# One RWKV-7 / gMLP layer: TensorE's sequence in the pair rounds fixed as the program traces it, with stated delays

## The chip, the cores and the metric

The kernel runs on one core of a Trainium2 chip, in one launch. The metric is the time of one execution on the device in microseconds (us). Two runs of the kernel before took 1193.26 and 1194.86 us, median 1194.06.

## What is computed

One layer of a decoder is applied to 512 prompt rows and 8 x 4 sample rows (544 rows in all, 1024 channels). Cut to what matters here:

```
xn   = rmsnorm(h);  proj = xn @ w_in            # columns [r | k | v | u | v_g | gate_A | gate_B], 7168 in all
r,k,v = token-shift mix of the first 3072 columns
decay, a, g = low-rank (LoRA) products of token-shifted xn
kk   = k * k_k / |k * k_k| (per head);  k = k * (1 + (a - 1) * k_a)
per head (16 of 64 channels), per row:          # RWKV-7 scan
    sa = S @ -kk;  S = S * w + sa (x) (kk * a) + v (x) k;  y = S @ r
o_A  = (head_norm(y) + sum(r * k * r_k) * v) * g
o_B  = gelu(u) * chunk_mix(layernorm(gelu(v_g)))
h   += rmsnorm((sigmoid(gate_A) * o_A + sigmoid(gate_B) * o_B) @ w_out)
h   += rmsnorm(relu(rmsnorm(h) @ w_up)^2 @ w_down);  h += sigmoid(h @ w_pg) * (p @ w_pe)
```

## The kernel before, in words

Channels lie on the 128 partitions and rows along the free axis, as eight tiles of 128 channels. A **dense** product (`dense`, L209 to 215, matmul at L214) of one 128x128 weight tile column with 544 rows is made in two halves of up to 296 and 258 columns. Each of 8 k-steps takes three matmuls: weights and rows are both split in a high and a low part (`xh`, `xl`, `w_hi`, `w_lo`; L188 to 193). A dense tile is thus 48 matmuls. `wload` (L195) reads its weights by SyncE and splits them on ScalarE (L191) and VectorE (L192).

The scan works on **pairs of heads**, p = 0 to 7, one tile of 128 channels each, and on eight chunks of 64 rows. These are the stages, each a Python generator that yields an estimate of its TensorE time:

- `front(p)` (L395 to 549): the dense k, r and v tiles (`rkv`, L321), the inverse norm of k per head, the LoRA products, exponentials, and the chunk products M (`L486`), BKT, ZV (the "products").
- `solve(p)` (L605): inverts each chunk's triangular matrix by 28 dependent VectorE steps between small products. scr (M to DRAM, L504), Xi (back, L612), solved (L623) and XD (L627) go through DRAM.
- `chain(p)` (L677): the scan over the chunks; each needs the last. A chunk is three hops: px = ZV^T M (L687), copied as Xc by ScalarE (L691); TT^T Xc (L701), read by ScalarE (L702) and VectorE (L703) into ZV; BKT^T ZV (L706), read by VectorE (L717) into the next chunk's ZV. L689 and L707 collect the outputs in py.
- `samples(p)` (L552): the sample rows, in small products.
- `back(p)` (L727): head norm of the output Y, gate g. `gates(p)` (L755): two dense gate tiles, and the result's sum. `mlp_u(j)` (L998): the dense u tiles.

A per-head sum is two matmuls with 0/1 weights on a split operand (`head_sum`, L339; matmuls L349, 350). `head_inverse` (L353) takes such sums as two rows, sends them by DMA to 64 partitions (st, L361, GpSimd's queue), takes 1/sqrt there and sends the result back (invk for k, invy for the head norm, L369, GpSimd's queue); `head_spread` (L373, matmul L377) spreads it over the heads' channels by two matmuls.

In **round** p (loop at L1111, p from -1 to 8) `weave` (L813) interleaves chain(p), samples(p), solve(p+1), front(p+2), back(p-1) and the gates that GATES names, always taking the generator that is furthest behind its share of the round in SPAN. That gives the program's order, and each instruction's priority. The tile scheduler then orders every engine's instructions itself, from priorities and its own estimates of when operands are ready. "Small products" below are matmuls of 64 rows or columns or less, which use a part of TensorE's array.

```
        def weave(*items):
            ...
            while live:
                x = min((x for x in live if len(x[2]) < 5 or x[2][4]()), key=lambda x: x[0])
```

After the rounds, w_out, w_up, w_down and w_pg follow as dense products.

Of the kernel before, what the change touches and what calls it, by code (L numbers as in the profile page):

```python
# [9 lines left out]
F32 = mybir.dt.float32  # L10
# [17 lines left out]
EARLY = ()  # L28

SPAN = {"chain": (0, 0.55), "samples": (0.1, 0.8), "solve": (0.05, 1.2), "front": (0, 1), "u": (-0.05, 1.04),  # L30
        "back": (-0.1, 0.5), "gates": (0, 1), "mixed": (0.4, 0.83), "front0": (0.1, 1.15), "mix": (0.3, 0.8),
        "u0": (0.1, 1.09)}
# [111 lines left out]
def _program(tc, a, o):  # L144
    nc = tc.nc
    act, dve, pe, sp, gp = nc.scalar, nc.vector, nc.tensor, nc.sync, nc.gpsimd
    from contextlib import ExitStack
# [38 lines left out]


# [108 lines left out]
    with tc.tile_pool(name="dr", bufs=1, space=DRAM) as dr:  # L296
# [24 lines left out]
        def rkv(kind, p, pad=0):  # L321

            w = wload(a["win"][8 * "rkv".index(kind) + p])
            t = ew.tile([128, 640 if pad else NT], F32, name=kind, tag=kind, bufs=2 if kind == "k" else 1)
            pa, pb = pd("d"), pd("d")
            dense(pa[:, 0:296], w, X, (0, 296))
            dense(pb[:, 0:258], w, X, (294, 552))
# [9 lines left out]
            return t  # L337

        def head_sum(x, sel, m, ring, tag):  # L339

            out = []
            for c0, c1 in (SA, SB):
# [5 lines left out]
                p_ = pd(ring)[0:m, 0:n]  # L348
                pe.matmul(p_, lhsT=sel, rhs=hi[:, 0:n], start=True, stop=False)  # L349
                pe.matmul(p_, lhsT=sel, rhs=lo[:, 0:n], start=False, stop=True)  # L350
                out.append(p_)
            return out

        def head_inverse(pool, sq, norm, tag, ring):

            rows = ew.tile([2, NT], F32, name="rows", tag="rows", bufs=1)
            for (c0, c1), p_ in zip((SA, SB), head_sum(sq, selw, 2, ring, tag)):
                act.copy(out=rows[:, c0:c1], in_=p_)  # L358
# [36 lines left out]
        def front(p):  # L395
            s = S[p]
            k = rkv("k", p)
            yield 5.6
            sq = ew.tile([128, NT], F32, name="sq", tag="tmp", bufs=1)
            act.activation(out=sq, in_=k, func=AF.Square, scale=vcol("k_k", p))  # L400
            inv = head_inverse(ew, sq, (1e-24, ALU.max, 1.0, ALU.mult), "k", "s")
# [39 lines left out]
            yield 1  # L441

# [5 lines left out]
            yield 1  # L448
            if p == 0:
# [24 lines left out]
            r_ = rkv("r", p)  # L474
            yield 5.6
# [4 lines left out]
            yield 0.5  # L480

# [9 lines left out]
            yield 3.5  # L491
# [18 lines left out]
            BKT = pair_tile(p, "BKT", [128, 8, 128], 2)  # L510
            for c in range(0, 8, 4):
# [4 lines left out]
                act.copy(out=BKT[:, c:c + 4], in_=p_.rearrange("p (c t) -> p c t", c=4))  # L516
            BKTs = ew.tile([128, 64], F32, name="BKTs", tag="BKTs", bufs=2)
# [5 lines left out]
            v = rkv("v", p, 32)  # L523
            yield 5.6
            ZV = pair_tile(p, "ZV", [128, 9, 2, 64], 2)
            SV = ew.tile([128, 64], F32, name="SV", tag="SV", bufs=2)
            for c in (0, 4, 8):
# [7 lines left out]
                else:  # L535
# [3 lines left out]
                    else:  # L539
                        act.copy(out=ZV[:, 0:3, 1], in_=q_[:, 1:4, 1])  # L540
                if c == 0:
# [3 lines left out]

            sv = pair_tile(p, "sv", [128, NT], 3)
            for (c0, c1), p_ in zip((SA, SB), head_sum(r_, blk, 128, "s", "v")):
                dve.tensor_tensor(out=sv[:, c0:c1], in0=p_, in1=v[:, 32 + c0:32 + c1], op=ALU.mult)
            yield 1
            s.update(F=Fp, KR=KR, M=M, scr=scr, BKT=BKT, ZV=ZV, sv=sv, KRs=KRs, Ms=Ms, BKTs=BKTs, SV=SV, Fs=Fs)  # L550

# [822 lines left out]
```

## Time and profile before

| | before |
|---|---|
| median of 2 runs | 1194.06 us |
| the profiled execution | 1195.11 us, its span 1193.3 us |
| before pair 0's front | 0 to about 95 us of the span |
| the rounds | about 95 to 690 us |
| w_out to the end | about 690 to 1193 us |
| TensorE, VectorE, ScalarE busy | 97%, 68%, 49% |

Busy shares are of the whole span. Durations of matmuls in the trace are from a matmul's start to its modelled end, which can lie past the start of the next; distances of starts tell how many a stretch can hold. Rows are those of the profiled execution, whose own time is the one to set a sum against.

### The profile page before, as it was taken

The numbers are of one execution on the slowest core, as the hardware profiler recorded it, in microseconds if no ns is written. First come the engines' busy times: TensorE is split into PE (matmuls) and PEld (weight loads), VectorE is DVE, ScalarE is ACT, GpSimd is POOL, SyncE is SP. The second block draws the span as 40 slices with busy tenths as digits, with TensorE's granted clock in tenths as the row PEclk, the third lists the DMA queues.
The fourth block names the chain that finished last, engine by engine and source line by source line (L and its number), as shares of the span: only waits on it lengthen the run. The fifth ranks groups of instructions, "written<-read, shape, count | busy, mean of one in ns | idle before, by whom it ended". The sixth has DMA issues, their size and how long they took to land.

```text
span 1193.3 us, 26307 instructions
## 1 busy us (share of the span) xinstructions
PE 1159.7 (97%) x10262; PEld 1086.1 (91%) x10262; DVE 815.6 (68%) x2251; ACT 579.7 (49%) x1406; POOL 108.0 (9%) x199
## 2 busy tenths in 40 slices
PE   7999998999899999999999999999999999999998
PEld 7999997888788888888878998999999999999998
DVE  6795778687878888887876646844563464465584
ACT  6646336557474747464655546642232232233352
POOL 0000012202230221122110000000000000000000
PEclk9999999999999999999999999999999999999999
DMA  6243253211222123141331452222222222222322
GB/s 203 72 126 114 100 159 114 86 50 46 63 74 83 48 64 99 34 118 44 112 95 55 131 171 72 91 81 89 88 89 89 89 89 89 89 89 89 116 73 83
DMA packets 68236, 109.33 MB, mean 92 GB/s; under 512 B 13712, under 2 KB 19760, under 8 KB 68112
## 3 DMA queue, kind: packets, MB, share of 16 engines
q1 hardware_dynamic: 60224, 103.94, 27.6%
q0 software_dynamic: 7600, 3.50, 1.8%
q8 instruction: 81, 1.33, 0.5%
q14 instruction: 43, 0.35, 0.1%
q10 hardware_dynamic: 288, 0.21, 0.1%
HBM read 94.40 MB, written 13.00 MB: 90 GB/s over the span
## 4 chain that ended last, share of the span: by engine, by line
PE 72%; DVE 12%; DMA 7%; ACT 6%; issue 2%; SPq 1%; POOL 0%; DVEq 0%; ACTq 0%; POOLq 0%
PE ps_d L214 47%; PE ps_s L214 3%; PE ps_s L486 2%; PE ps_b L214 2%; PE ps_m L214 2%; DVE w_lo L192 2%; ACT w_hi L191 2%; PE ps_cx L687 1%; PE ps_cx L701 1%; PE ps_cx L706 1%; DMA w_raw<-in_wout 1%; DMA w_raw<-in_wpg 1%; PE ps_cy L707 1%; DVE KR L456 1%; PE ps_m L601 1%
## 5 line engine op out<-in xcount | busy, mean ns | idle before, releaser
L192 DVE TENSOR_TENSOR w_lo<-w_raw,w_hi 128x512 fp32r<-128x512 f32 (+1 forms) x288 | 195.5, 681 | 174.0 <-ACT w_hi L191 169.9
L191 ACT CAST w_hi<-w_raw 128x512 fp32r<-128x512 f32 (+1 forms) x288 | 176.2, 613 | 275.9 <-PE ps_d L214 190.1
L214 PE MATMUL ps_d<-xh,w_hi 128*128 128x256 f32 (+3 forms) x832 | 249.4, 300 | 3.5 <-ACT w_hi L191 2.5
L214 PE MATMUL ps_d<-xl,w_hi 128*128 128x256 f32 (+3 forms) x832 | 246.9, 297 | 0.0
L214 PE MATMUL ps_d<-xh,w_lo 128*128 128x256 f32 (+3 forms) x832 | 246.9, 297 | 0.0
L214 PE MATMUL ps_d<-hh,w_hi 128*128 128x288 f32 (+1 forms) x1200 | 227.7, 288 | 0.0
L214 PEld LDWEIGHTS ps_d<-hh,w_hi 128*128 128x128 f32 x1200 | 188.8, 188 | 0.0
L214 PE MATMUL ps_d<-hh,w_lo 128*128 128x288 f32 (+1 forms) x600 | 173.6, 289 | 0.0
L214 PEld LDWEIGHTS ps_d<-xh,w_hi 128*128 128x128 f32 x832 | 157.5, 189 | 7.5 <-ACT w_hi L191 2.9
L214 PEld LDWEIGHTS ps_d<-xl,w_hi 128*128 128x128 f32 x832 | 157.6, 189 | 4.0 <-issue 3.2
L214 PEld LDWEIGHTS ps_d<-xh,w_lo 128*128 128x128 f32 x832 | 157.1, 189 | 2.2 <-issue 0.8
L214 PE MATMUL ps_d<-ax,w_hi 128*128 128x288 f32 (+1 forms) x704 | 133.3, 288 | 0.0
L214 PEld LDWEIGHTS ps_d<-hh,w_lo 128*128 128x128 f32 x600 | 112.8, 188 | 0.2 <-DVE w_lo L192 0.2
L214 PEld LDWEIGHTS ps_d<-ax,w_hi 128*128 128x128 f32 x704 | 110.3, 188 | 0.4 <-issue 0.2
L214 PE MATMUL ps_d<-ax,w_lo 128*128 128x288 f32 (+1 forms) x352 | 101.5, 288 | 0.0
L214 PEld LDWEIGHTS ps_d<-ax,w_lo 128*128 128x128 f32 x352 | 66.2, 188 | 0.0
L1256 ACT ACTIVATE ax<-t 128x288 fp32r<-128x288 f32 (+1 forms) x64 | 27.5, 430 | 45.4 <-DVE t L1255 45.2
L214 PE MATMUL ps_d<-gx,w_hi 128*128 128x288 f32 (+1 forms) x192 | 41.4, 309 | 6.8 <-ACT gx L853 6.0
L697 ACT ACTIVATE ZP<-ZV,Fp 64x64 f32<-64x64 f32 x96 | 33.1, 345 | 20.7 <-DVE ZV L717 17.3
L214 PEld LDWEIGHTS ps_d<-gx,w_hi 128*128 128x128 f32 x192 | 32.3, 199 | 8.1 <-ACT gx L853 6.0
L1257 DVE TENSOR_TENSOR t<-t 128x288 f32<-128x288 f32 (+1 forms) x64 | 28.1, 439 | 15.7 <-ACT ax L1256 15.3
L361 POOL DMA_DIRECT2D st<-rows x32 | 16.2, 511 | 243.9 <-ACT rows L358 176.8
(455 smaller groups left out, 2295.4 us busy)
## 6 DMA issues: line engine op xcount, KB each, us to landing
w_raw<-in_win SPq DMA_DIRECT2D x112, 256.0 KB, 2.8
w_raw<-in_wup SPq DMA_DIRECT2D x64, 256.0 KB, 2.7
w_raw<-in_wdn SPq DMA_DIRECT2D x64, 256.0 KB, 2.8
w_raw<-in_wout SPq DMA_DIRECT2D x16, 256.0 KB, 3.1
w_raw<-in_wpg SPq DMA_DIRECT2D x16, 256.0 KB, 2.9
w_raw<-in_lora SPq DMA_DIRECT2D x10, 256.0 KB, 2.8
xt<-in_xt SPq DMA_DIRECT2D x8, 276.0 KB, 5.4
ud<-u SPq DMA_DIRECT2D x8, 272.0 KB, 2.2
```

The costliest lines, as they stand in the source:

```text
L191: act.copy(out=hi, in_=raw)
L192: dve.tensor_tensor(out=lo, in0=raw, in1=hi, op=ALU.subtract)
L214: pe.matmul(out, lhsT=w[wi][k - k0], rhs=x[xi][k][:, cols[0]:cols[1]], start=start and n == 0 and j == 0, stop=stop and n == len(ks) - 1 a ...
L361: gp.dma_start(out=st[32 * h:32 * h + 32], in_=rows[h:h + 1].rearrange("o (a b) -> o a b", b=17))
L456: dve.tensor_tensor(out=KR[r, :, 0, h], in0=c3(kk)[r], in1=E[r, :, 0:64], op=ALU.mult)
L486: pe.matmul(p_[:, 256 * ci:256 * ci + 256], lhsT=BK[:, c + ci].rearrange("p a t -> p (a t)"), rhs=KR[:, c + ci].rearrange("p a h t -> p (a ...
L601: pe.matmul(p_[r], lhsT=s["BKTs"][r], rhs=SX[r], start=True, stop=True)
L687: pe.matmul(px[:, 0:128], lhsT=flat(M[:, c, 0]), rhs=flat(ZV[:, c]), start=True, stop=True)
L697: act.activation(out=ZP[r], in_=zv[h][r], func=AF.Copy, scale=F[r, c + 1, 0:1])
L701: pe.matmul(px[:, 0:128], lhsT=TT[:, c], rhs=Xc, start=True, stop=True)
L1256: act.activation(out=hi, in_=t, func=AF.Square)
L1257: dve.tensor_tensor(out=t, in0=t, in1=t, op=ALU.mult)
```

## The change

1. TensorE's instructions in the rounds are taken from the tile scheduler: `tc.manual_schedule(engines={PE})` keeps them in the order in which the program emits them. The other engines are still ordered by the scheduler; the chain's instructions get high priority there.
2. A class `Clock` stands in for TensorE while the program is traced and adds up an estimated time. Generators may yield `(cost, delay)`: `weave` resumes them only when that clock has passed the delay. HOP, 1.5 us, is the delay after each hop of the chain and the samples.
3. All dense tiles of the rounds come from one stream, `tiles()`, two k-steps (six matmuls, `dense_by`) at a time. Weights are loaded one tile ahead. `weave` emits a dense piece when the round's quota of tiles is behind the furthest-behind ready generator, or when no generator is ready. In front, back and gates the dense tiles are no longer inside the generator; `until` waits for what a tile or another generator sets.
4. `products` is split from `front` and emitted one round later. `head_sum` puts 3 us between its split and its matmuls, with one at a time under way (`held`). The spread of invk is held 11 us, that of invy 17; solve's steps 6, 14, 7 and 3 us.
5. rows -> st goes by ScalarE's queue in place of GpSimd's. u tiles 4 and 5 stand in round -1, 6 and 7 in rounds 6 and 7.

```diff
-EARLY = ()
+U = {-1: (4, 5), 6: (6,), 7: (7,)}
+HOP = 1.5
+    class Clock:
+        def matmul(self, out, lhsT, rhs, **kw):
...
+            self.now += t + (0.17 if small != self.small else 0)
+            return nc.tensor.matmul(out, lhsT=lhsT, rhs=rhs, **kw)
+    pe = Clock()
+    def dense_by(out, w, x, cols, by=2):
+        for k in range(0, KT, by):
+            dense(out, w, x, cols, ks=range(k, k + by), k0=0, start=k == 0, stop=k + by == KT)
+            yield 0.37 * by
+        def until(q, what):
+            while q >= 0 and not S[q].get(what):
+                yield 0, 0.3
-        def head_sum(x, sel, m, ring, tag):
+        def head_sum(x, sel, m, ring, done):
+            while held[0]:
+                yield 0, 0.2
+            held[0] = True
...
+            yield 0, 3
+            held[0] = False
...
-                gp.dma_start(out=st[32 * h:32 * h + 32], in_=rows[h:h + 1].rearrange("o (a b) -> o a b", b=17))
+                act.dma_start(out=st[32 * h:32 * h + 32], in_=rows[h:h + 1].rearrange("o (a b) -> o a b", b=17))
         def front(p):
-            k = rkv("k", p)
-            yield 5.6
+            yield from until(p, "k")
+            k = s["k"]
...
+            yield 0, 11
             ia, ib = head_spread(inv, "s")
...
+            s.update(F=Fp, KR=KR, sv=sv, BK=BK, BR=BR, Fs=Fs, front=True)
+        def products(p):
+            yield from until(p, "front")
...
         def chain(p):
                 act.copy(out=Xc, in_=px[:, 0:128])
-                yield 0.7
+                yield 0.7, HOP
...
         def back(p):
-            inv = head_inverse(ewb, sq, (1.0 / 64, ALU.mult, 64e-5, ALU.add), "y", "b")
-            yield 6
+            inv = yield from head_inverse(ewb, sq, (1.0 / 64, ALU.mult, 64e-5, ALU.add), "y", "b")
+            yield 6, 17
...
+        def weave(quota, *items):
+            live = [[it[2], (it[3] - it[2]) / cost.get(it[0], 40.0), it, 0.0] for it in items]
+            base, end = wide["done"], wide["due"] + quota
+            wide["due"] = end
+            while live or (end == len(TILES) and wide["done"] < end):
+                can = [x for x in live if x[3] <= pe.now]
+                x = min(can, key=lambda x: x[0]) if can else None
+                at = (wide["done"] - base) / max(0.5, end - base)
+                if wide["done"] < len(TILES) and (x is None or at < x[0]) and wide["wait"] <= pe.now:
+                    c = next(wide["tiles"], None)
...
+                    continue
+                if x is None:
+                    pe.now = min([x[3] for x in live] + ([wide["wait"]] if wide["done"] < len(TILES) else []))
+                    continue
+                    with tc.high_priority() if x[2][0] in FIRST else nullcontext():
+                        c = next(x[2][1])
+                    c, after = c if isinstance(c, tuple) else (c, 0.0)
+                    x[3] = pe.now + after
+        def tiles():
+            w = wload(src(*TILES[0]))
+            for i, (x, j) in enumerate(TILES):
+                ahead = wload(src(*TILES[i + 1])) if i + 1 < len(TILES) else None
+                yield from mlp_u(w, j) if x == "u" else gate(w, x, j) if isinstance(x, int) else rkv(w, x, j)
+                w = ahead
+        order = tc.manual_schedule(engines={mybir.EngineType.PE})
```

In the changed kernel every TensorE instruction is issued at L205 (the matmul of `Clock`); line numbers of the other engines shift: st is L411, the inverses' transfers L419, scr L572, Xi L680, solved L691 and XD L695. Three places show how the change moves instructions. Dense matmuls have output `ps_d`.

The first place is TensorE in the first hop of pair 4's chunk 4 (round 4), from the chunk's first product to TT^T Xc. Before:

```order
L687 MATMUL ps_cx<-ZV,M 128x128
L689 MATMUL ps_cy<-KR,ZV 128x128
L214 MATMUL ps_d<-xl,w_hi 128x296
L214 MATMUL ps_d<-xh,w_lo 128x296
L701 MATMUL ps_cx<-Xc,TT 128x128
```

In the changed kernel, the first of the dense pieces between them and the last rows of the hop:

```order
L205 MATMUL ps_cx<-ZV,M 128x128
L205 MATMUL ps_cy<-KR,ZV 128x128
L205 MATMUL ps_d<-xh,w_hi 128x296
L205 MATMUL ps_d<-xl,w_hi 128x296
L205 MATMUL ps_d<-xh,w_lo 128x296
...
L205 MATMUL ps_b<-invy,selt 128x288
...
L205 MATMUL ps_cx<-Xc,TT 128x128
```

Two dense matmuls stood in this hop; now twelve do (six ahead of the spread of invy, six behind it).

The second place is TensorE in chunk 4 of the last pair, 7, whose chain ends the rounds. Before, its first two hops:

```order
L687 MATMUL ps_cx<-ZV,M 128x128
L214 MATMUL ps_d<-xh,w_hi 128x288
L689 MATMUL ps_cy<-KR,ZV 128x128
L214 MATMUL ps_d<-xl,w_hi 128x288
L701 MATMUL ps_cx<-Xc,TT 128x128
L214 MATMUL ps_d<-xh,w_lo 128x288
L214 MATMUL ps_d<-xh,w_hi 128x288
...
L706 MATMUL ps_cx<-ZV,BKT 128x128
```

In the changed kernel, the whole chunk:

```order
L205 MATMUL ps_cx<-ZV,M 128x128
L205 MATMUL ps_cy<-KR,ZV 128x128
L205 MATMUL ps_cx<-Xc,TT 128x128
L205 MATMUL ps_b<-invy,selt 128x288
L205 MATMUL ps_cx<-ZV,BKT 128x128
L205 MATMUL ps_cy<-M,ZV 128x128
L205 MATMUL ps_b<-invy,selt 128x256
L205 MATMUL ps_cx<-ZV,M 128x128
```

The dense matmuls between the hops are gone: the stream's last tile stands within pair 7's first chunk.

The third place is GpSimd's queue in a round. Before:

```order
L504 DMA scr<-M 32x8x32 x4
L612 DMA Xi<-scr 32x16x16 x2
L361 DMA st<-rows 32x1x17 x4
L369 DMA invy<-q 1x32x17 x4
L369 DMA invk<-q 1x32x17 x4
L623 DMA solved_153<-Xi 32x16x16 x2
L627 DMA XD<-solved_153 32x8x32 x4
```

In the changed kernel:

```order
L572 DMA scr<-M 32x8x32 x4
L419 DMA invk<-q 1x32x17 x4
L419 DMA invy<-q 1x32x17 x4
L680 DMA Xi<-scr 32x16x16 x2
L691 DMA solved_154<-Xi 32x16x16 x2
L695 DMA XD<-solved_154 32x8x32 x4
```

st has left this queue for ScalarE's, and Xi stands behind both inverses' transfers, where it stood directly behind scr.

## Rows read from the trace of the kernel before

**Rows 1.** The page's head: span; each engine's busy us, share and instructions.

```profile
span 1193.3 us, 26307 instructions
...
PE 1159.7 (97%) x10262; PEld 1086.1 (91%) x10262; DVE 815.6 (68%) x2251; ACT 579.7 (49%) x1406; POOL 108.0 (9%) x199
```

**Rows 2.** Windows: stretch, length, PE, PEld, DVE, ACT, POOL, granted clock, DMA share, GB/s.

```profile
332.20:582.10 249.90, 242.42 (x2523) 212.98 (x2522) 208.36 (x687) 147.29 (x417) 54.34 (x98) 1.00 0.26 74
627.30:658.20 30.90, 30.58 (x269) 25.57 (x268) 20.36 (x64) 16.77 (x50) 2.98 (x6) 1.00 0.17 53
```

**Rows 3.** Lines of TensorE, 332.2 to 582.1: busy us, mean ns, idle before.

```profile
L214 PE MATMUL ps_d<-xl,w_hi 128*128 128x296 f32 (+3 forms) x306 | 91.6, 300 | 0.0
...
L486 PE MATMUL ps_s<-KR,BK 128*128 128x256 f32 x64 | 16.4, 387 | 0.5 <-DVE BK L471 0.3 <-DVE M L488 0.2
L701 PE MATMUL ps_cx<-Xc,TT 128*128 128x128 f32 x64 | 14.5, 308 | 0.3 <-ACT Xc L691 0.2
...
L567 PE MATMUL ps_m<-BR,Z 64*64 64x8 f32 x128 | 4.7, 200 | 0.0
```

**Rows 4.** The chain of waits, dense stretch behind the rounds: start, us, what.

```profile
811.83 81.25 PE ps_d L214 x648
```

**Rows 5.** Timeline of TensorE near 300 us: start, us, engine, line, operation.

```profile
299.84 0.27 PE L706 MATMUL ps_cx<-ZV,BKT 128*128 128x128 f32 x1
299.95 0.39 PE L707 MATMUL ps_cy<-M,ZV 128*128 128x128 f32 x2
300.26 0.30 PE L582 MATMUL ps_m<-ysub,Ms 32*32 32x64 f32 x4
300.50 0.41 PE L214 MATMUL ps_d<-xh,w_lo 128*128 128x296 f32 x1
```

**Rows 6.** Timeline, one chunk of pair 7's chain.

```profile
641.97 0.38 PE L687 MATMUL ps_cx<-ZV,M 128*128 128x128 f32 x2
642.39 0.27 ACT L691 COPY Xc<-ps_cx 128x128 f32<-128x128 f32 x1
642.77 0.43 PE L701 MATMUL ps_cx<-Xc,TT 128*128 128x128 f32 x2
...
643.77 0.49 PE L706 MATMUL ps_cx<-ZV,BKT 128*128 128x128 f32 x2
644.29 0.60 DVE L717 SCALAR_TENSOR_TENSOR ZV<-ps_cx,Fp,ZP 64x64 f32<-64x64 f32 x2 [0.58 <-PE ps_cx L706]
...
645.04 0.35 PE L687 MATMUL ps_cx<-ZV,M 128*128 128x128 f32 x1
```

**Rows 7.** Timelines of GpSimd and TensorE, one inverse norm and the Xi before it.

```profile
393.87 1.29 POOL L612 DMA_DIRECT2D Xi<-scr  x2 [3.11 <-DMA scr<-M]
...
403.94 0.28 PE L350 MATMUL ps_s<-hs_lo,selw 128*2 128x256 f32 x1
...
408.21 0.99 POOL L361 DMA_DIRECT2D st<-rows  x2 [3.43 <-ACT ZV L702]
...
416.92 1.95 POOL L369 DMA_DIRECT2D invk<-q  x4 [1.96 <-PE ps_d L214]
...
430.85 0.41 PE L377 MATMUL ps_s<-invk,selt 128*128 128x288 f32 x2
```

**Rows 8.** View of the tile invk: its transfers.

```profile
DMA to landing us min/median/max: 1.5/1.7/3.9
```

**Rows 9.** Timeline, the end of the rounds.

```profile
658.05 0.42 PE L706 MATMUL ps_cx<-ZV,BKT 128*128 128x128 f32 x2
...
679.93 0.29 PE L377 MATMUL ps_b<-invy,selt 128*128 128x288 f32 x1
...
685.74 0.28 PE L751 MATMUL ps_b<-GT,l2hi 96*128 96x256 f32 x1
...
689.57 0.73 DVE L793 SCALAR_TENSOR_TENSOR hh<-cm,hh 128x544 fp32r<-128x544 f32 x1 [0.72 <-ACT hh L792]
```

**Rows 10.** Windows, one microsecond of round 6; columns as in rows 2.

```profile
624.00:625.00 1.00, 1.00 (x7) 1.00 (x6) 0.55 (x2) 0.64 (x2) 0.00 (x0) 0.50 0.86 320
```

More of the change, by code (lines that the diff above doesn't have):

```diff
@@ L27 @@
 GATES = {2: (0,), 3: (1,), 4: (2,), 5: (3,), 6: (4,), 7: (5,), 8: (6, 7)}
-EARLY = ()
-SPAN = {"chain": (0, 0.55), "samples": (0.1, 0.8), "solve": (0.05, 1.2), "front": (0, 1), "u": (-0.05, 1.04),
-        "back": (-0.1, 0.5), "gates": (0, 1), "mixed": (0.4, 0.83), "front0": (0.1, 1.15), "mix": (0.3, 0.8),
-        "u0": (0.1, 1.09)}
+U = {-1: (4, 5), 6: (6,), 7: (7,)}
+SPAN = {"chain": (0, 0.97), "samples": (0.1, 0.9), "products": (-0.1, 0.1), "solve": (0.1, 0.95), "front": (0, 1),
+        "u": (0, 1), "back": (-0.1, 0.6), "gates": (0, 1), "mixed": (0.4, 0.83), "front0": (0.1, 1.0), "mix": (0.3, 0.8),
+        "u0": (0.1, 1.0)}
+FIRST = ("chain",)
+HOP = 1.5
 KAPPA = float(0.5 * np.exp(-0.5))
@@ L448, in front @@
             yield 1
+            yield from until(p - 1, "products")
             if p == 0:
@@ L473, in front @@
             yield 1
[L474 to L475 removed]
+            yield from until(p, "r")
+            r_ = s["r"]
             for h, r in enumerate(HS):
@@ L544, in front @@
             yield 1
[L546 to L550, printed above, removed]
+            s.update(M=M, scr=scr, BKT=BKT, ZV=ZV, KRs=KRs, Ms=Ms, BKTs=BKTs, SV=SV, products=True)
         def samples(p):
@@ L590, in samples @@
                                                  op1=ALU.subtract)
+                yield 0.5, HOP + (1.5 if it == 2 else 0)
+            SX = ewb.tile([128, NB, 64], F32, name="SX", tag="SX", bufs=1)
+            dve.tensor_tensor(out=SX, in0=SV.unsqueeze(1).broadcast_to([128, NB, 64]),
+                              in1=C["maskb"][:, 0:8].unsqueeze(2).broadcast_to([128, NB, 64]), op=ALU.mult)
+            yield 0, 3
             p_ = pd("m")
@@ L752, in back, with gate @@
                 dve.tensor_tensor(out=Y[:, c0:c1], in0=Y[:, c0:c1], in1=p_[:, 0:n], op=ALU.mult)
+                yield (0.5, 1.5) if c0 == 0 else 0.5
             s["done"] = True
+        def gate(w, col, p):
+            t = ewb.tile([128, NT], F32, name="gt", tag="gt", bufs=2)
+            for (c0, c1), x in zip((SA, SB), (XA, XB)):
+                p_ = pd("d")
+                yield from dense_by(p_[:, 0:c1 - c0], w, X, x)
+                act.activation(out=t[:, c0:c1], in_=p_[:, 0:c1 - c0], func=AF.Tanh, scale=0.5)
+            S[p][col] = t
         def gates(p):
@@ L825, in weave @@
             cost.update(spent)
+        TILES = [("k", 0), ("u", 0), ("r", 0), ("u", 1), ("v", 0), ("u", 2), ("u", 3)]
+        QUOTA = [len(TILES)]
+        for p in range(-1, 9):
+            t = [[(x, p + 2) for x in "krv"] if p < 6 else [], [("u", j) for j in U.get(p, ())],
+                 [(c, q) for q in GATES.get(p, ()) for c in (48, 40)]]
+            t = [x for part in t[0:1] + [t[1] + t[2]] for x in [part]]
+            TILES += [x for i in range(4) for part in t for x in part[i:i + 1]]
+            QUOTA.append(sum(map(len, t)))
+        def tiles():
+            src = lambda x, j: a["win"][{"r": 0, "k": 8, "v": 16, "u": 24}.get(x, x) + j]
+            w = wload(src(*TILES[0]))
[3 more added lines that the diff above has]
+                w = ahead
+        wide = {"done": 0.0, "due": 0, "wait": 0.0, "tiles": tiles()}
         late_stack = ExitStack()
@@ L1096, in each @@
                 yield from fn(j)
-        weave(("front", front(0), *SPAN["front0"]), ("mix", chunk_mix(), *SPAN["mix"]), ("u", each(mlp_u, range(0, 4)), *SPAN["u0"]))
+        order = tc.manual_schedule(engines={mybir.EngineType.PE})
+        order.__enter__()
+        weave(QUOTA[0], ("front", front(0), *SPAN["front0"]), ("mix", chunk_mix(), *SPAN["mix"]))
         late_stack.close()
```

190 lines of the change are left out of this document (103 added, 87 removed).

## The prediction, made before the changed kernel had run

> **What bounds the kernel now.** I read the page first, then the windows by round, then the lines of TensorE in four rounds, then single chunks, and the other queues where something moved. The page shows TensorE busy 97% of the span [rows 1], but a matmul's record lasts past the next one's start and so covers short waits too. I therefore price its work by the distance of starts. A long run of dense matmuls takes 81.25 us for 648, 0.125 us each [rows 4], as a mean over halves of 288 and 256 columns. A float32 product of 128 columns is recorded as two passes; L707 follows L706's second by 0.11 us [rows 5].
>
> Four whole rounds take 249.9 us [rows 2]. In them stand three groups of 306, 306 and 305 dense matmuls [rows 3]: 917 x 0.125 = 115.0 us. There are 144 other single-pass matmuls of the head sums, spreads and LoRA products: 18.0. Passes of 128 columns number 388 (L701's 64 is the first group [rows 3]): 42.7. The 64 of L486 [rows 3] have 256 columns, 0.22 each: 14.1. Ten groups of small products, L567's 4.7 us the largest [rows 3], are busy 28.9 in all. The sum is 218.7, so 31.2 us, **7.8 per round**, is TensorE waiting, though the windows show only 249.9 - 242.4 = 7.5 us of it as idle. VectorE is busy 208.4 of the same 249.9 us, 83% [rows 2]. These rounds are bound by TensorE plus short waits, with VectorE close behind.
>
> Where the waits are shows in one chunk of the scan. In its shortest, 3.07 us [rows 6], Xc is copied out of PSUM by ScalarE before L701 can start, 0.80 us after L687; L706 waits for VectorE's L703, 1.00 us; the next L687 for L717, 1.27 us. In the order before, often only two dense matmuls and L689 stand in the first of these hops.
>
> **The change part by part.** All terms are against the profiled execution, 1195.1 us, of which 1193.3 are its span [rows 1]; it lies 0.1% above the median, 1194.06. Before pair 0's front and behind the last round nothing moves.
>
> *Fewer switches.* A block of small products costs when it is entered and left: L707's two passes need 0.22 us, yet L582 starts 0.31 after it, and the next dense matmul 0.24 after L582's tiny four [rows 5]. I take 0.22 per block. The orders hold 125 such blocks before and 97 now: **-6**, between -3 and -9.
>
> *Longer hops in the chains of pairs 0 to 6.* I summed for all 64 chunks the TensorE work that stands in each hop, at the prices above, and set it against the shortest chunk's hops [rows 6]. Pairs 0 to 6 are short of them by 12 us before and by 4 now. With 0.2 us more per hop, one short VectorE or ScalarE instruction ahead in the queue, it is 31 and 6; with 0.3 us, 42 and 8. The change gives -8 to -34. In the typical chunk an instruction is ahead, so I take **-22**.
>
> *Other waits.* About half of the 7.8 per round is not the chain's: first passes whose weights load only when the wait ends, head sums that wait for their low halves. Head sums are now held 3 us and products follow their front by most of a round. 6.5 rounds at 3.9 are 25 us; this edit could give 0 to -25. I take **-10**.
>
> *Weights one tile ahead, gating products and u tiles elsewhere.* A dense tile is 48 matmuls, 6.0 us, and its load is issued a tile earlier; I cost this at nothing while VectorE and ScalarE split it within those 6 us. If they don't, the next tile waits and the 0.7 us splits are what is late.
>
> *The inverse norms.* The 32 transfers of rows leave GpSimd's queue for ScalarE's. In the order before they stood behind others: L350 ends the sums at 403.94, rows go out at 408.21, the first of four invk transfers at 416.92, issued over 1.95 us, and they land 1.7 us later [rows 7, 8]: 16.6 us, hidden since the spread stands at 430.85, 26.9 later. Now it stands 10.3 us of TensorE's work behind the sums, some 11.3 with its own waits. Everything behind it on TensorE, the chain included, then waits with it. At the old pace that is 5.3 us in each of 7 rounds, 37; at nothing late, 0. The 4.3 us before rows' issue should nearly vanish, which leaves 12.3 against 11.3, so I take **+6**. ScalarE spends at most what GpSimd does, 0.5 us each [rows 7], 16 us over the rounds, and is 59% busy [rows 2]: hidden.
>
> *The solve.* Its Xi load stood directly behind scr (393.87 [rows 7]) and is now queued behind both inverses' transfers. The first product that needs it stands 35 us of work behind the products, so I cost it at nothing; if VectorE's 28 dependent steps are late it adds to the inverse's wait, up to 5 us a round, kept for a rival.
>
> *The last chain.* This is the loss. Dense tiles fill every hop earlier in the program, and they end within pair 7's first chunk. Behind it stand, to the chain's end, 70 passes (7.7), 21 single-pass matmuls (2.6) and four small blocks (1.1): 11.4 us, while seven chunks need 21.5 at the shortest [rows 6] and 27.0 at this round's mean of 30.9 / 8 [rows 2]. That leaves 10 to 16 us of waits, where 30.9 us at 7.8 per 62.5 had 4 before: +6 to +12. VectorE has less to do there, 20.4 of 30.9 us [rows 2]: **+7**.
>
> *The last back.* From chain 7's last product (658.05) to the spread of the inverse at 679.93 went 21.9 us [rows 9], under dense gate tiles and w_out. Now 13.1 us of work stands there: 0 to 9 late, I take +6, since some of the 21.9 was queueing. From the last LoRA product (685.74) to the last hh half (690.30) are 4.6 us [rows 9], with 2.1 of work left: +2.5. Together **+8.5**.
>
> Sum: -6 - 22 - 10 + 6 + 7 + 8.5 = -16.5, and 1195.1 - 16.5 = **1179**.
>
> **The clock** is a price the sum leaves out. After two blocks of small products the granted clock stood at 0.50, 1.2 of 2.4 GHz, in the microsecond from 624 on [rows 10]. The bare end of chain 7 is more of the same. The Trainium skill, page "TensorE: Matmul & The Clock Gate", section "HAM oscillation — how this bites in real kernels", says that idle gaps put the gate back to half rate and the next matmuls start cold; by that rule the end would run at half clock, and the fall at 624 agrees.
>
> **The rivals.**
> - *All short waits go* (1153). Switches -6, 7 of the 7.8 us in 6.5 rounds and the start -48, the end +12, no wait for inverses. For it: distances of 1.5 to 2.5 us now stand where 1.0 to 1.3 are needed. Against: VectorE at 83%.
> - *VectorE takes over* (1194). If rounds shrink by 5 us, VectorE is 52 of 57 us busy, and each hop waits in its queue. Then only 10 us are gained from chains and the switches' 6 stay, against the end's 15.5: 1195.1 - 16 + 15.5.
> - *The end at half clock* (1187). Each of 21 bare hops has two passes more by 0.11 us, 4.6, and some 3 us of dense work follow at double time: +8 on the forecast.
> - *Slower* (1229): an inverse or a solve that lands late blocks TensorE, whose order no longer steps aside. At 8 us in each of 7 rounds, 56 in place of 6, it is 1179 + 50. It decides from (1218 - 1173) / 7 = 6.4 us a round on, a landing later than 17.7 us after the sums; [rows 7] has 16.6.
>
> That the change does nothing can be left out: the orders differ in every round.
>
> **How the numbers follow.** Forecast 0.36; all waits gone 0.26; VectorE 0.17; half clock 0.12; slower 0.09. Two per cent, about what a measurement of this kernel can tell from no change, is below 1170 or above 1218. Faster takes the second case and a little of the first's lower side: 0.31. Slower is 0.09, same the remaining 0.60. The range, 1155 to 1206, takes in most of the first four cases and the hops' bounds.
>
> **What would show it.** Right: rounds of pairs 1 to 6 shorter by 4 to 6 us each; chain 7 with chunks of 3.0 to 3.5 us and idle TensorE; waits of some microseconds for invy just ahead of the last hh products. Wrong: gaps before the invk spreads or the XN products in every round, VectorE above 90%, or a chain 7 no longer than now.

## The result and the profile after

The changed kernel takes 1316.75 us (2 runs, 1315.29 to 1318.21) against 1194.06: **10.3% slower**, ratio 1.1028 with a 95% interval of 1.0966 to 1.1089. The forecast was 1179, the range 1155 to 1206, the slower rival 1229: the sign was wrong and the size lay outside everything considered. One run of the kernel before, at a granted clock of 0.655, took 1548.5 us and stands in no comparison; in every profiled run named below the clock of the last 480 us, behind the rounds, is 0.99 or above.

The page's head and its rows of TensorE and of the granted clock, in 40 slices of the span; they answer to [rows 1]:

```profile
span 1316.4 us, 26310 instructions
...
PE 1204.6 (92%) x10262; PEld 1129.5 (86%) x10262; DVE 822.5 (62%) x2251; ACT 589.5 (45%) x1409; POOL 91.7 (7%) x167
...
PE   7999899888887979888799988999999999999998
...
PEclk9999599986898989989899958999999999999999
```

The instructions are the same, the engines' busy time nearly so; the loss is in slices 4 to 25, counted from 1 (99 to 823 us), the rounds. The last half of hh, which ends them, came at 690.30 before [rows 9]:

```profile
817.32 0.72 DVE L870 SCALAR_TENSOR_TENSOR hh<-cm,hh 128x544 fp32r<-128x544 f32 x1 [0.72 <-ACT hh L869]
```

It ends at 818.04: the rounds are 127.7 us longer, and what follows 4.6 shorter. Where in the rounds: pair 0's first product came 15.9 us later than before (236.4 for 220.5), pair 1's 26.3 later, pair 2's 48.0, pair 6's 98.6, pair 7's 121.2. The rounds up to pair 6 lose; the bare last chain, which I took for the loss, adds only 6.5. A stretch of TensorE's sequence without a dense matmul is called **bare** below.

The same four rounds as in [rows 2], chain of pair 2 to chain of pair 6; then four stretches with little or no dense work: `chunk_mix` ahead of pair 0, the longest bare stretch (the end of pair 0's chain and the start of pair 1's), the start of pair 3's round, and pair 7's chain from its second chunk on; columns as there:

```profile
380.20:680.70 300.50, 254.82 (x2569) 227.90 (x2565) 213.00 (x688) 153.91 (x419) 44.75 (x80) 0.93 0.23 65
133.00:163.00 30.00, 24.80 (x87) 19.06 (x85) 13.01 (x39) 0.74 (x2) 0.00 (x0) 0.55 0.23 83
286.00:327.00 41.00, 32.60 (x343) 25.41 (x342) 20.67 (x71) 21.12 (x63) 6.34 (x12) 0.63 0.10 25
457.00:479.70 22.70, 18.45 (x130) 13.76 (x129) 16.57 (x58) 14.65 (x45) 3.89 (x8) 0.85 0.25 73
757.00:792.00 35.00, 29.24 (x111) 21.19 (x112) 16.88 (x57) 11.98 (x38) 1.99 (x4) 0.51 0.09 29
```

300.5 us against 249.9, for the same work. TensorE is visibly idle for 45.7 of them, where it was 7.5; VectorE's share falls from 83% to 71%, so it isn't the bound. The bare stretches run at a mean clock of 0.51 to 0.85. What TensorE waits for in the four rounds, the four longest (engine, line, releaser: us, times, longest):

```profile
PE ps_d L205 <- DVE v L378: 17.0, 4, 4.2
PE ps_s L205 <- ACT F L471: 7.1, 8, 1.2
PE ps_s L205 <- ACT rows L408: 5.0, 8, 0.9
PE ps_s L210 <- DVE Ms L564: 2.9, 4, 1.3
```

The first is one wait per round. TensorE's timeline of one:

```profile
488.37 0.28 PE L205 MATMUL ps_d<-xh,w_lo 128*128 128x258 f32 x1
492.89 0.61 PE L205 MATMUL ps_d<-xh,w_hi 128*128 128x296 f32 x1 [4.24 <-DVE v L378]
493.30 0.45 PE L205 MATMUL ps_d<-xl,w_hi 128*128 128x296 f32 x1
493.55 0.45 PE L205 MATMUL ps_d<-xh,w_lo 128*128 128x296 f32 x1
```

and VectorE's over the same time:

```profile
486.48 1.39 DVE L514 SCALAR_TENSOR_TENSOR BK<-ta,kk 64x512 f32<-64x512 f32 x2
...
488.98 1.39 DVE L523 TENSOR_TENSOR BK<-k,F 64x512 f32<-64x512 f32 x2
...
490.51 0.78 DVE L531 SCALAR_TENSOR_TENSOR r<-r,vec,k 128x544 f32<-128x544 f32 x1
...
492.37 0.47 DVE L378 SCALAR_TENSOR_TENSOR v<-ps_d,vec,v 128x255 f32<-128x255 f32 x1
```

The next dense tile needs the PSUM bank that v's reads empty. They stand in VectorE's queue behind the front's work, and TensorE, whose next rows were fixed, does nothing for 4.24 us. Then it runs at half rate: its dense matmuls start 0.25 us apart; [rows 4] gives 0.125. The windows show the clock before, in and behind that wait:

```profile
487.00:488.00 1.00, 1.00 (x10) 1.00 (x10) 0.95 (x3) 0.37 (x1) 0.00 (x0) 1.00 0.00 0
491.00:492.00 1.00, 0.00 (x0) 0.00 (x0) 1.00 (x6) 0.68 (x2) 0.00 (x0) 0.50 0.00 0
494.00:495.00 1.00, 1.00 (x6) 1.00 (x6) 1.00 (x5) 0.00 (x0) 0.00 (x0) 0.50 0.00 0
```

The granted clock is 1.00, 2.4 GHz, ahead of the wait, 0.50, 1.2 GHz, in it and behind it. The Trainium skill, page "TensorE: Matmul & The Clock Gate", section "HAM oscillation — how this bites in real kernels", says that idle gaps put the gate back to half rate and the next matmuls start cold; this wait agrees.

**An account of the rounds.** From 66 us to the last hh I set the distance of each pair of starts against the prices of the prediction. What exceeds them is, in microseconds at half clock, the price a second time ("half"), and for the rest waiting, put to the engine that the trace names as the last releaser. Distances shorter than the price are set against "waits" but not against the three columns behind it, which therefore add up to some 25 us more.

| | last hh | work | half | waits | for VectorE | for ScalarE | none named |
|---|---|---|---|---|---|---|---|
| before | 690.3 | 561.5 | 1.1 | 61.6 | 18.8 | 14.5 | 53.9 |
| changed | 818.0 | 560.5 | 51.0 | 140.6 | 74.7 | 42.3 | 45.4 |

Of 127.7 us, 49.9 are work at half clock and 79.0 are waits. In stretches of over 3 us between two dense matmuls, the rounds before the first w_out product hold 68 us (63 of work) before and 277 us (137 of work) now: 139 us of the 277 are not work, where 5 of the 68 were not. That is as much as the whole loss; beside dense work TensorE loses nothing more than before.

### The profile page after: what moved, and what is told of

The parts are those of the page before. It is cut to its first block, busy times and chain, and to the rows that moved or that the text cites. A ratio compares the mean times of both kernels' runs of the same rounds, so it can differ in the third digit from the quotient of the medians.

```text
span 1316.4 us, 26310 instructions
## 1 busy us (share of the span) xinstructions
PE 1204.6 (92%) x10262; PEld 1129.5 (86%) x10262; DVE 822.5 (62%) x2251; ACT 589.5 (45%) x1409; POOL 91.7 (7%) x167
## 5 line engine op out<-in xcount | busy, mean ns | idle before, releaser
L205 PE MATMUL ps_d<-xh,w_hi 128*128 128x296 f32 (+3 forms) x848 | 264.1, 313 | 20.8 <-DVE v L378 18.4
L205 PE MATMUL ps_d<-xl,w_hi 128*128 128x296 f32 (+3 forms) x848 | 249.9, 296 | 0.0
L205 PE MATMUL ps_d<-xh,w_lo 128*128 128x256 f32 (+3 forms) x832 | 245.8, 295 | 0.0
L205 PE MATMUL ps_d<-hh,w_hi 128*128 128x288 f32 (+1 forms) x1200 | 228.4, 288 | 0.1
L205 PEld LDWEIGHTS ps_d<-hh,w_hi 128*128 128x128 f32 x1200 | 188.9, 188 | 0.3 <-ACT hh L869 0.3
L205 PEld LDWEIGHTS ps_d<-xh,w_hi 128*128 128x128 f32 x848 | 165.6, 196 | 24.4 <-DVE v L378 19.4
L205 PE MATMUL ps_d<-hh,w_lo 128*128 128x288 f32 (+1 forms) x600 | 173.2, 289 | 0.0
L205 PEld LDWEIGHTS ps_d<-xl,w_hi 128*128 128x128 f32 x848 | 165.5, 196 | 0.1
L205 PEld LDWEIGHTS ps_d<-xh,w_lo 128*128 128x128 f32 x832 | 162.1, 195 | 0.0
L205 PE MATMUL ps_d<-ax,w_hi 128*128 128x288 f32 (+1 forms) x704 | 133.2, 288 | 0.0
L205 PEld LDWEIGHTS ps_d<-hh,w_lo 128*128 128x128 f32 x600 | 112.8, 188 | 0.0
L205 PEld LDWEIGHTS ps_d<-ax,w_hi 128*128 128x128 f32 x704 | 110.3, 188 | 0.2 <-issue 0.2
L205 PE MATMUL ps_d<-ax,w_lo 128*128 128x288 f32 (+1 forms) x352 | 101.5, 288 | 0.0
L205 PEld LDWEIGHTS ps_d<-ax,w_lo 128*128 128x128 f32 x352 | 66.2, 188 | 0.0
L1360 ACT ACTIVATE ax<-t 128x288 fp32r<-128x288 f32 (+1 forms) x64 | 27.5, 430 | 45.4 <-DVE t L1359 45.1
L205 PE MATMUL ps_d<-gx,w_hi 128*128 128x288 f32 (+1 forms) x192 | 41.1, 308 | 6.8 <-ACT gx L969 6.2
L205 PE MATMUL ps_s<-KR,BK 128*128 128x256 f32 x128 | 42.4, 463 | 4.3 <-ACT F L471 4.3
L767 ACT ACTIVATE ZP<-ZV,Fp 64x64 f32<-64x64 f32 x96 | 33.0, 344 | 27.7 <-DVE ZV L787 23.5
L205 PEld LDWEIGHTS ps_d<-gx,w_hi 128*128 128x128 f32 x192 | 32.3, 199 | 7.8 <-ACT gx L969 6.2
```

Source lines behind the costliest of these rows:

```text
L205: return nc.tensor.matmul(out, lhsT=lhsT, rhs=rhs, **kw)
L767: act.activation(out=ZP[r], in_=zv[h][r], func=AF.Copy, scale=F[r, c + 1, 0:1])
L1360: act.activation(out=hi, in_=t, func=AF.Square)
```

## The experiments

e13, e14, e16 and e17 are timed in several rounds; the others are one profiled run each, beside runs of the kernel before of 1191 to 1204 us. Small effects among the latter, some 5 us, are not told apart. The theories that the expectations name by letters are explained where each is first named.

**Is it TensorE's fixed sequence?** e1 gives the order of the changed program back to the scheduler:

```diff
-        order = tc.manual_schedule(engines={mybir.EngineType.PE})
+        order = nullcontext()
```

> The changed program with TensorE's order given back to the tile scheduler; nothing else differs. Theory A (the fixed sequence is what costs: it has stretches with no dense matmul in them, in which TensorE can only wait and its clock falls to half): the scheduler pulls dense tiles into the waits, time 1190 to 1240, mean granted clock 0.98 or more, against 1316.8 and 0.935. Rival B (the program's order itself, with products at once at a round's start and the dense stream run ahead, is what costs, whoever orders TensorE): 1270 to 1320, clock 0.96 or less.

Measured: 1356.4, clock 0.919. Theory A fell, it seemed: the scheduler was 40 us slower with this program. e6 fixes the sequence of the kernel before as its program has it (the same context around its calls of weave):

> The kernel before with TensorE's sequence fixed as its own program has it, and nothing else changed. By the order its chain hops are short by 86 us of what the shortest chunk needs, and 181 us of work stand in stretches over 2 us without a dense matmul. If a fixed sequence is only as good as the program's mixing: 1370 to 1480, clock 0.92 or less. If fixing costs little by itself (with the changed program the fixed sequence was 40 us faster than the scheduler's): 1220 to 1300.

Measured: 1524.5, clock 0.862; a fixed sequence without stated delays is worse than I gave it. To a fixed sequence the change's other edits are worth some 200 us.

**Is it the delays or the mixing?** e2 drops the delays, e5 changes the rule that places dense pieces:

```diff
-                    x[3] = pe.now + after
+                    x[3] = pe.now + (after if after <= 0.3 else 0.0)
```

> The changed kernel without its stated delays (all over 0.3 us count as 0). By the order, work of TensorE in stretches without a dense matmul falls from 109 to 55 us (prices of the prediction). Theory A (the delays make weave pull dense tiles ahead and leave the rest bare): bare stretches took 277 us for 137 of work, so half of the loss, some 60 us, comes back, less some 20 for hops that are now short: 1255 to 1285. Rival (the delays are what hides the hops): slower than 1317. Rival (clock alone decides, short waits between dense tiles cost little): 1220 to 1255, clock 0.97 or more.

Measured: 1356.7; bare stretches 287 us in place of 289 (to the last hh), though the order promised half. The waits went to other releasers, here the inverse's transfer:

```profile
PE ps_s L205 <- DMA invk<-q: 21.3, 4, 7.4
PE ps_s L205 <- ACT hs_hi L393: 16.5, 8, 2.4
```

Without the delays the inverse, which the changed kernel waited for once (0.5 us in all), is waited for four times: there the delays do hide what they state.

```diff
-                if ... (x is None or at < x[0]) ...
+                est = {n: cost.get(n, 40.0) for n in spent}
+                part = sum(min(spent[n], est[n]) for n in est) / sum(est.values())
+                if ... (at < part + (LEAD if x is None else 0) or wide.get("stuck", 0) > 2 * len(live)) ...
```

> The changed kernel with another rule in weave: a dense piece goes out whenever the dense stream's share of its round is behind the other generators' summed share, and runs ahead by at most 0.3 while all are held. Work in stretches over 2 us without a dense matmul falls from 109 to 61 us by the order (53 in the kernel before); the delays stay. Theory C (clusters of small stages, in which TensorE's products wait for VectorE and ScalarE while no dense tile is left beside them, cost the 139 us): 1225 to 1275, clock 0.97 or more. Rival D (VectorE's work comes in a backlog each round, whoever stands beside it on TensorE): 1295 or more, with named waits for VectorE as before, 70 us.

Measured: 1325.7. Bare stretches fell to 233 us, waits for VectorE rose from 75 to 89. Theory C fell: with the sequence fixed, dense work moved next to the small work does not cover the waits.

**Is it the clock?** e3 fills the hops of the bare last chain:

```diff
+        def filler(p, c, n):
+            if p == 7 and 1 <= c:
+                f_ = pd("d")
+                for j in range(n):
+                    pe.matmul(f_[:, 0:288], lhsT=blk, rhs=X[0][j % KT][:, 8:296], start=True, stop=True)
...
                 act.copy(out=Xc, in_=px[:, 0:128])
                 yield 0.7, HOP
+                filler(p, c, 6)
```

> In pair 7's chunks 1 to 7 each hop gets 6, 7 or 9 added dense matmuls (256 x 128 x 288 operands at hand, result unused), 0.8, 0.9 and 1.2 us of work at full clock, 154 in all, 20 us. Their chunks took 4.07 to 6.68 us each in the changed kernel, at half clock. If the lost clock makes them long: the clock stays at 1.0, chunks take 3.3 to 4.2 us, the stretch gets shorter by some 8 us although 20 us of work is added. If waits for other engines make them long: the added work hides and nothing changes, within 2 us. If TensorE's own work does: longer by 15 to 20.

Measured: 1317.8. The window that was at 0.51 in the changed kernel (the last of the windows by stretch above) has, with the filler:

```profile
757.00:792.00 35.00, 32.84 (x250) 30.53 (x250) 17.80 (x60) 12.29 (x36) 1.99 (x4) 1.00 0.11 33
```

Full clock, 139 more matmuls recorded in the same 35 us, and seven chunks take 40.0 us in place of 38.9. The sum is nothing, within the 2 us stated, but two things can make it: a clock that costs nothing, or added work that takes what the clock gives back. One hop without other work, at half clock in the changed kernel, then a hop with the filler at full clock:

```profile
787.36 0.77 PE L205 MATMUL ps_cx<-ZV,M 128*128 128x128 f32 x2 [0.35 <-DVE ZV L787]
788.16 0.27 ACT L761 COPY Xc<-ps_cx 128x128 f32<-128x128 f32 x1 [0.67 <-PE ps_cx L205]
788.48 0.80 PE L205 MATMUL ps_cx<-Xc,TT 128*128 128x128 f32 x2
```

```profile
781.64 0.38 PE L205 MATMUL ps_cx<-ZV,M 128*128 128x128 f32 x2
782.00 1.04 PE L205 MATMUL ps_d<-xh,blk 128*128 128x288 f32 x6
782.06 0.27 ACT L767 COPY Xc<-ps_cx 128x128 f32<-128x128 f32 x1 [0.60 <-PE ps_cx L205]
782.88 0.39 PE L205 MATMUL ps_cx<-Xc,TT 128*128 128x128 f32 x2
```

ScalarE's copy starts 0.80 us after its product at half clock and 0.42 at full clock, so the clock does cost. But with the filler the next product starts 0.55 us after the copy's end, directly behind the sixth filler: there TensorE's own work holds the chain, as it does in nearly every filled hop. A chunk without other work takes 4.07 us in the changed kernel (783.29 to 787.36), 4.02 with the filler (781.64 to 785.66) and 3.07 at its shortest in the kernel before [rows 6]. By an estimate from these times the half clock costs up to 1.0 us a chunk, some 7 us over seven, and the added work took them back. For the other stretches, with 42 of the 51 us of "half", no run tells cost from symptom.

**Is it one queue or one wait?** e4 gives the PSUM reads of k, r and v high priority (`with tc.high_priority():` around the two activations and the `scalar_tensor_tensor` of `rkv`).

> The reads of the k, r and v tiles out of PSUM get high priority on ScalarE and VectorE, so VectorE takes v's ahead of the front's work that stood before them (4.2 us of idle TensorE in each of four rounds, half clock behind each). If VectorE's queue is the cause: the waits for v fall from 18.4 us to under 9, and with the half clock behind them the kernel is 10 to 25 us faster. If the bank or the tile v comes free late for another reason: no change, within 5 us.

Measured: 1319.6. TensorE's waits in the four rounds are now:

```profile
PE ps_m L205 <- DVE Y L666: 12.2, 4, 3.1
PE ps_s L205 <- ACT F L472: 6.3, 8, 1.2
PE ps_m L205 <- DVE XN L701: 5.6, 4, 1.8
```

The wait for v is gone, and TensorE waits as long for what now stands behind v and the front's work on VectorE, L666 and L701 (L665 and L700 in the changed kernel, where they had 1.2 and 0.8 us in these rounds). e7 takes four operations of each front off VectorE, e8 does so in the kernel before:

```diff
-                dve.tensor_tensor(out=BK[r, :, 1 - h], in0=c3(k)[r], in1=F[r, :, 1:65], op=ALU.mult)
+                gp.tensor_tensor(out=BK[r, :, 1 - h], in0=c3(k)[r], in1=F[r, :, 1:65], op=ALU.mult)
-                dve.tensor_tensor(out=KR[r, :, 1, h], in0=c3(r_)[r], in1=E[r, :, 1:65], op=ALU.mult)
+                gp.tensor_tensor(out=KR[r, :, 1, h], in0=c3(r_)[r], in1=E[r, :, 1:65], op=ALU.mult)
```

> In the changed kernel four tensor_tensor of each front (k x F into BK, r x E into KR, 64 x 512 each, 0.7 us each on VectorE) go to GpSimd, which has little to do and whose results are needed a round later. Theory D (VectorE's backlog in the stretch before the v tile is what TensorE waits for): 2.8 us and the half clock behind it in each of 7 rounds, 20 to 35 us: 1282 to 1297. If the waits come from each chain of dependent steps and not from the queue: 1310 to 1320. If GpSimd takes over 3 us for each: slower, to 1340.

> The same four operations moved to GpSimd in the kernel before, whose rounds have VectorE busy for 83% and TensorE waiting for 7.8 us each. If short VectorE queues are part of these waits: 1 to 2 us per round, 1180 to 1188. If not: 1190 to 1195. If GpSimd's longer operations come late for the products, which there follow in the same round: slower, 1200 to 1215.

Measured: 1341.6 and 1212.8, both slower. This does not test VectorE's queue: 32 operations of 21.8 us left it in e7, and yet VectorE was busy for 829.5 us in place of 822.5, because other operations took longer beside GpSimd's (last section). e10 and e11 undo two more edits: weights loaded at each tile's own start (`w = wload(src(x, j))` in `tiles`), and solve's transfers by `sp.dma_start`.

> The changed kernel with each dense tile's weights loaded in the program at its own start and not one tile ahead; TensorE's sequence is the same. In four rounds VectorE waited 23 us at the head of its queue for ScalarE's w_hi, ScalarE 18 for TensorE's release of the weight buffers. If that early load is what blocks the queues: 1270 to 1300. If not: 1305 to 1325. If the split then comes late for each tile, 1 to 2 us for 50 tiles: 1350 to 1420.

> The changed kernel with the solve's three groups of transfers (Xi, solved, XD) issued by SyncE, past GpSimd's queue of inverses. In four rounds VectorE stood 12.5 us at the head of its queue for XD. If that wait is a cause: 3 us a round and what hangs on it, 1275 to 1300. If VectorE would only wait elsewhere: 1310 to 1322. If SyncE's own waits hold the transfers up: slower.

Measured: 1317.1 and 1328.1. Neither is a cause. Loading ahead costs nothing, as the prediction had it.

**The chain's priority.** e9 keeps TensorE's sequence, e12 gives it to the scheduler; both have

```diff
-FIRST = ("chain",)
+FIRST = ()
```

> The changed kernel with the chain's high priority on ScalarE and VectorE taken away; TensorE's sequence is the same, row for row. In four rounds of the changed kernel ScalarE stood at the head of its queue waiting for the chain's products for 46 us (ZV and Xc; 10 in the four rounds before), with what TensorE waits for (F, rows, SV, v) behind. Theory E (the chain's instructions stand too early in the queues of ScalarE and VectorE and block what TensorE needs next): 10 us and more per round with the half clock: 1200 to 1270, TensorE's named waits for ScalarE and VectorE under 60 us in place of 113. Rival D (VectorE's work as such): 1300 to 1330. Rival: the chain's hops get longer instead: slower, 1320 to 1360.

> The changed program with TensorE given to the scheduler as in e1_free_order (1356), and without the chain's high priority. Theory E: what made that run slower than the kernel before was the chain standing too early in every queue; by the order its hops are now short by 14 us of what the shortest chunk needs, not 40: 1200 to 1260, clock 0.98 or more. Rival (the products a round later and the single dense stream are what costs in either order): 1300 to 1360.

Measured: 1298.2 and 1239.2. With the sequence fixed the priority costs 19 us, less than theory E wanted, and ScalarE's waits for the chain hardly moved (22.7 and 19.3 for ZV and Xc, from 23.5 and 22.5). In the scheduler's order it costs 117, and e12 lies in theory E's range, though its clock, 0.967, is lower than expected: e1 was slow through the priority, and had hidden what the fixed sequence costs. Without the priority that is e9 less e12, **59 us**. So theory A comes back.

**What the tiles' place is worth, in either order.** e13 holds the dense stream to 1.15 of the round's quota, e14 is e5's rule; both in the scheduler's order without priority. e15 is e13 with the sequence fixed.

```diff
-                if ... (x is None or at < x[0]) ...
+                if ... (at < 1.15 if x is None else at < x[0]) ...
```

> As e12_free_no_priority (1239: scheduler's order, no priority for the chain), and weave no longer takes dense pieces beyond 1.15 of a round's quota when every generator is held. In that run the rounds up to the last dense matmul end at 677 us, as in the kernel before (678), but what stands behind it took 42 us in place of 12 and the start of w_out 14 more at half clock. Theory F (the delays let the dense stream run ahead, and the bare end is nearly all of what the changed program costs in the scheduler's order): 1188 to 1208. Rival G (products a round later cost in every round): 1222 to 1245.

> As e12_free_no_priority with the rule of e5_even in weave (dense share kept level with the other generators' share), which also keeps dense tiles to the end; by the order its chain hops are short by 10 us of what the shortest chunk needs (15 in the kernel before), and 53 us of work stand in bare stretches, as before. Theory F: 1186 to 1210. Rival G: 1222 to 1245. If the mixing is the better one within the rounds too: below 1186.

> The rule of e13 with TensorE's sequence fixed, without the chain's priority (e9: 1298). If the bare end costs there as in the scheduler's order, some 30 to 40 us less: 1255 to 1270, and the rest of the way to e13 is what a fixed sequence costs by itself, 55 to 65 us. If the fixed sequence turns the tiles' new place into other waits (hops short by 21 us in place of 13): 1285 to 1320.

Measured: e13 1216.3 (ratio to before 1.0174, 1.0144 to 1.0204), e14 1204.8 (1.0059, 1.0031 to 1.0087), e15 1335.7. e12 was 47 us over its own run of before, e13 is 21 and e14 10 over the median of theirs: keeping tiles to the end takes away 26 of the 47, and e14's rule, which also mixes differently within the rounds, 37. e13 lies between the theories, and F holds for that part. The same rule makes the fixed sequence slower, 1298 to 1336; that its tiles had been covering waits there is likely, not shown.

e16 and e17 move u tiles (e16 `U = {-1: (4,), 0: (5,), 1: (6,), 6: (7,)}`, e17 `U = {-1: (4,), 0: (5,), 6: (6,), 7: (7,)}`, in e14), e18 fixes the sequence of e16.

> As e14_even_free (1205, rounds over at 690.3 us of the span as before) with the u tiles 4 to 7 in rounds -1, 0, 1 and 6 in place of -1, -1, 6 and 7: in that run rounds 0 to 2 had one stretch from 250 to 325 us with 43 us bare for 28 of work, 24 of them at half clock. By the order the longest bare stretch falls from 14.4 to 5.0 us. If dense tiles beside the small work are what decides: 10 to 17 us less, 1183 to 1196. If the stretch comes from the first chain's own waits: 1200 to 1210.

> As e16_even_free_u with u tile 6 in round 6 and 7 in round 7 (rounds -1, 0, 6, 7), hops short by 9.3 in place of 10.6 us. If the tiles' place in rounds 0 to 1 decides, half of the gain of e16: 1188 to 1200; if the end of the rounds does, the better of the two: 1183 to 1192.

> e16_even_free_u with TensorE's sequence fixed, and nothing else: what fixing costs with the best mixing found. By the order 54 us of work stand bare and hops are short by 18 us, near the kernel before, so if the order of TensorE alone decided it would be within 20 us of e16. If a fixed order is bound to wait where ScalarE and VectorE, in orders of their own, are late: 60 to 120 us above e16, 1250 to 1310, with 60 us and more of named waits for VectorE.

Measured: e16 1234.6 (1.0325, 1.0298 to 1.0352), e17 1209.7 (1.0128, 1.0109 to 1.0146), e18 1318.5. Both missed: fewer bare stretches by the order made nothing faster, and why e16 is 30 us slower than e14 stays open. e18 says what was asked: 84 us more for fixing alone. The accounts, as above, each to its last hh (that of e6 is a recount with one mean price for the small products, which meets the others within 2 us):

| program | scheduler's order: time, waits for VectorE, for ScalarE | fixed: the same |
|---|---|---|
| before | 1194; 19, 14 | e6 1524; 172, 63 |
| changed, no priority | e12 1239; 32, 26 | e9 1298; 68, 40 |
| capped, no priority | e13 1216; 36, 20 | e15 1336; 89, 49 |
| even, u moved, no priority | e16 1235; 33, 20 | e18 1318; 94, 36 |

TensorE's longest waits in four rounds of e12, and of e18:

```profile
PE ps_s L205 <- ACT hs_hi L393: 6.9, 2, 3.5
PE ps_b L205 <- DVE Y L812: 3.4, 1, 3.4
```

```profile
PE ps_cx L206 <- DVE ZV L774: 15.8, 5, 5.5
PE ps_m L206 <- DVE Y L666: 6.8, 4, 3.3
PE ps_cx L206 <- DVE ZV L788: 5.0, 3, 4.0
```

Three versions of the changed program, one edit, 59 to 120 us, and each time the waits for VectorE double or more: the longest for v in e9 (17.1 us in four rounds), for ZV and Y in e18. In the program of before, which states no delays, they rise from 19 to 172 and the time by some 330. No version beat the kernel before; e14 came nearest.

## Why the prediction was wrong

The ladder of the loss, by runs: 1194 before; 1239 with the changed program in the scheduler's order without priority (+45); 1298 with its sequence fixed (+59); 1317 with the chain's priority (+19). The last two steps don't add in another order: with the priority first they are +117 and -40.

- **"Longer hops in the chains" and "Other waits", -22 and -10: this failed.** I counted the work standing in each hop and took it for cover. The step fails because that holds only if every other instruction of the fixed sequence is ready when its turn comes. In the changed kernel waits rose by 79 us, 56 of them for VectorE and 28 for ScalarE, while those without a named releaser fell by 8.5. The sum had left out (two rivals had a part of it, at other places and prices) that ScalarE and VectorE keep orders of their own: a read of v that stands behind the front's work in VectorE's queue stops TensorE and everything behind, where the order before had set other work there. e4 shows that moving one such read only moves the wait; e12 against e9, and the two pairs like it, show the price of the fixed sequence.
- **The premise of the end term failed too.** I wrote that dense tiles fill every hop before the last chain. They don't: in pairs 2 to 5 the last hop of chunk 0, all three of chunk 1 and the first two of chunk 2 hold no dense matmul, and pair 3's chunk 1 takes 13.7 us (462.6 to 476.3), 3.3 before. Each of these rounds begins with a stretch of products, sums and LoRA matmuls alone (22.7 us from 457.0, for 13.3 of work), and `chunk_mix`, which before stood among dense tiles (96 to 156 us), came in one piece. I had summed all work of TensorE hop by hop and not looked for runs without a dense row.
- **The last chain, +7, and the last back, +8.5:** chunks of pair 7 took 38.9 us for seven, 28.8 before, so +10, near the term by luck in part, since up to 7 of it is the half clock that the sum left out. From pair 7's first product to the last hh it is 69.5 us for 63.0: +6.5 for both terms together, where they add up to +15.5. In e12 keeping tiles to the end takes away over half of what the program costs (e13); in the changed kernel the end is the smaller part.
- **The inverse norms, +6, and the slower rival:** its effect was right (an order that no longer steps aside) and its place wrong. In the whole span TensorE waited once for invk and once for invy:

```profile
PE ps_b L205 <- DMA invy<-q: 3.1, 1, 3.1
...
PE ps_s L205 <- DMA invk<-q: 0.5, 1, 0.5
```

  Its condition, a landing later than 17.7 us after the sums, came true for three of the eight invk (17.9, 18.4 and 18.7 us), and still cost next to nothing: TensorE, held up by its other waits, reached these spreads 18.2 to 19.0 us after the sums, not 11.3. The time was 88 us above its 1229.
- **Fewer switches, -6:** no run tells it apart.
- **Weights one tile ahead, at nothing:** right (e10: 1317.1).
- **Half clock, +8 at the end:** sign and size were about right there (some 7 us, the estimate under e3) and the place incomplete: 50 us of the account are half clock, most of it in earlier rounds, in long bare stretches and behind every wait of over 2 us. The reading of 624 was wrong: just before that fall TensorE did small products and was idle for 0.17 and 0.48 us only, so it doesn't bear out a rule on idle gaps; the wait of 4.24 us does.
- **VectorE takes over:** it did not become the bound (71% busy), though most named waits are for it. A queue that is not full can be late.

What stays open: whether ScalarE's and VectorE's orders could be fixed to suit TensorE's, which was not tried, and how much of the 42 us at half clock outside the last chain is cost and how much only follows from waits.

## What to carry to other kernels

Cover in an order is only as good as the readiness of what stands ahead of it: before fixing one engine's sequence, look for what it waits for on engines that are still ordered by someone else, since any late read there now stops it. Look in the order for the longest runs without the work that needs nobody, and not only at the distance between dependent steps. When an experiment says that undoing a part makes things worse, look for a second part that works against it (here the priority) before dropping the theory. And work added to raise the clock shows only the sum of what the clock gives back and what the work takes; read the rows of a hop before calling either nothing.

## What the runs showed of the hardware

GpSimd took 1450 ns for L523's multiplication of 64x512 that VectorE does in 684, and VectorE's own L514, ten of whose 16 instances then ran beside it, went from 685 to 1073 ns in the mean. VectorE in the changed kernel, then VectorE in e7, then GpSimd in e7 (busy us, mean ns, idle before):

```profile
L514 DVE SCALAR_TENSOR_TENSOR BK<-ta,kk 64x512 f32<-64x512 f32 x16 | 11.0, 685 | 0.3
L523 DVE TENSOR_TENSOR BK<-k,F 64x512 f32<-64x512 f32 x16 | 10.9, 684 | 0.2
```

```profile
L514 DVE SCALAR_TENSOR_TENSOR BK<-ta,kk 64x512 f32<-64x512 f32 x16 | 17.2, 1073 | 0.3
```

```profile
L523 POOL TENSOR_TENSOR BK<-k,F 64x512 f32<-64x512 f32 x16 | 23.2, 1450 | 23.5 <-DVE k L521 23.0
```

The Trainium skill, "Perfetto Trace Analysis", "Optimizing Scalar/DVE Operations", warns that GpSimd and VectorE share a read port of SBUF, so that moving work between them may not help; here it cost 25 us in the changed kernel and, against its own run of before, 15 in the kernel before. And 20 us of dense work added to bare hops in e3 raised the granted clock there from 0.51 to 1.00 and left the time as it was, 1317.8 us: the clock gave back about what the work took.
